# Moving the retention key projection behind product y in the third mixer problem of a two-layer encoder trunk

## The chip, the cores and the metric

The kernel runs on one core of one Trainium2 chip. The metric is the device time of one execution in microseconds (us), the median over several runs. Each run also has a profiled sibling, an execution recorded by the hardware profiler, from which every row below is taken. The engines are PE (matrix products; PEld is its weight load), DVE, ACT, POOL and SP, which issues most of the DMAs.

## What is computed

A trunk of two layers works on `x` of 512 positions by 1024 channels, in float32. Each layer is a token mixer and a gated feed-forward network, each followed by a layer norm. The mixer multiplies `x` by one wide matrix `w_in` and uses its columns for three branches:

```
h = x @ w_in[l]
rq, rk, rv, rg, cq, ck, cv, dq, dk, dv, gates = split(h)
o_a = silu(rg) * rmsnorm(retention(rotary(rq), rotary(rk), rv))   # 4 heads, keys of 128, values of 256
o_b = chunk_attention(cq, ck, cv)                                 # 8 heads of 64
o_c = diff_attention(rotary(dq), rotary(dk), dv)                  # 4 heads
merged = sum(sigmoid(gate_i) * (o_i @ w_branch_i));  x = layer_norm(a*x + merged @ w_out)
```

The change concerns the stretch in which `rk` of heads 2 and 3 and `rv`, `rg` of heads 2 and 3 are projected while the retention of heads 0 and 1 is finished.

## The kernel before, in words

Each float32 operand is carried as two float32r parts, a high part (a cast) and a low part (the rest), and each product is three matmuls (`mm3`, lines 121 to 124): high by high, high by low, low by high. A weight block of 128x2048 is loaded into a staging tile `st`, cast by ACT into `wh` (line 259 for whole blocks, 154 for blocks split in two halves), and subtracted by DVE into `wl` (lines 260 and 155).

Three pairs of wide projections of the mixer are **problems** called `w`, `p` and `q` (line 1114): `w` makes the values of branches b and c, `p` makes `rv` and `rg` of heads 0 and 1, and `q`, the last one, those of heads 2 and 3. Each problem is done with seven block products in place of eight (class `Close`, line 219, and `u_two`, line 733). The products are `m1`, `y`, `v`, `m2`, `x`, `g` and `h`. Some accumulate onto another's PSUM banks: `v` onto `y`'s, and `x` and then `g` onto `m1`'s. Before that happens ACT copies the bank out (`copy`, line 747; line 750 in the profile, `tc<-pf`). Each product has two halves, j=0 and j=1, each in one PSUM bank and each of 12 matmuls.

The operand names in the profile tell the products apart: `s12` is read by `y` and `x`, `s43` by `v` and `g`, `xT` in a `pf` product by `m1`, `m2` and `h`. `pt<-xT` is a plain projection such as the key block `rk` (`u_rqk`, line 681: 24 matmuls for each of two heads, then the rotation of lines 378 to 387 and a split).

The weight blocks of a problem are sums of quarters of the matrix. Block `a` (used by `y`) and block `c` (used by `g`) are put together by an accumulating DMA well ahead. `v` loads a quarter `d`, makes its block from it, and then adds `a` to it on DVE (line 233); `x` uses the sum. `m2` loads `e` and adds `d` to it (line 239); `h` uses that.

The mixer's work is a hand-written list of **items** (lines 1115 to 1131). An item is a weight block with the code that uses it, and up to two groups of small jobs, the first run after j=0 and the second after j=1 (`between`, line 549). The jobs here are one head's share of the retention: `s_dh` loads a decay table, `s_r1` makes scores (`psr`), `s_r2` multiplies them by the values (`pro`, 30 matmuls into two banks) and scales the result (DVE lines 833 and 840, with a power on POOL in between), and `s_r3` transposes that (`prt`, two banks) and splits it into `oa` (ACT line 108, DVE line 114).

Four pools set who has to wait for whom: `st` has 4 tiles, `wh` and `wl` have 3 each, there are 8 PSUM banks, and 61 general tiles (`NSTAGE`, `AHEAD`, line 66, `NSLOT`). `run_items` (line 555) fetches the block of item i+2 when item i begins, so that a cast waits for the block of item i-1 to be read to its end.

The program is not run in the order of this text: a scheduler at build time writes one fixed order for each engine, in which the order of the text is a priority and free tiles count. On the chip each engine then goes through its own fixed order. The rows of the prediction show places in which that order differs from the list.

Of the kernel before, what the change touches and what calls it, by code (L numbers as in the profile page):

```python
# [35 lines left out]
RQ, RK, RV, RG, CQ, CK, CV, DQ, DK, DV, GATE = (  # L36
    0, 512, 1024, 2048, 3072, 3584, 4096, 4608, 5120, 5632, 6144)
# [19 lines left out]
def trunk(ctx, tc, x_in, xT_in, w_in, ret_norm_g, da_norm_g, lq1, lk1, lq2, lk2, w_a, w_b, w_c, b_merge, w_out,  # L57
# [19 lines left out]
    def g(dt=F32, name="g"):  # L77
        return gp.tile([P, 512], dt, tag="g", name=name)
# [4 lines left out]
    def bank(name="ps"):  # L83
        return psp.tile([P, 512], F32, tag="ps", name=name)
# [15 lines left out]
    def triangle(name):  # L100

        return [Pair(name), Pair(name), HalfPair(name)]
# [13 lines left out]
    def split(pr, src, cols=slice(None), scale=None):  # L116

        part_hi(pr.hi[:, cols], src, scale)
        part_lo(pr.lo[:, cols], src, pr.hi[:, cols], scale)
# [226 lines left out]
    def proj_T(act, wt, c0, nk=KT, ps=None, half=None):  # L346

        ps = bank("pt") if ps is None else ps
        sl = slice(0, S) if half is None else slice(256 * half, 256 * half + 256)
        for k in range(nk):  # L350
            a = act[k]
            mm3(ps[:, sl], wt.hi[:, k, c0:c0 + P], wt.lo[:, k, c0:c0 + P], a.hi[:, sl], a.lo[:, sl],
                k == 0, k == nk - 1)
        return ps
# [194 lines left out]
    def between():  # L549

        if pending:
            for fn in pending.pop(0):
                fn()
# [54 lines left out]
    def layer(l):  # L608
# [4 lines left out]
        def wcols(c, n):  # L613
            return W[:, c:c + n]

        v = {}
# [51 lines left out]
        rq, rk, rv, rgt = {}, {}, {}, {}  # L668
# [7 lines left out]
        def rqk_done(dst, h, ps):  # L676
            r = rotary(ps, tabs["cr"], tabs["sr"], 64)
            dst[h] = Pair("rqk")
            split(dst[h], r)

        def u_rqk(dst, base, hp):
            def fn(wt):
                for j in range(2):
                    rqk_done(dst, 2 * hp + j, proj_T(xT, wt, P * j))
                    between()
            return [([wcols(base + 256 * hp, 256)], KT)], fn
# [99 lines left out]
        def s_dh(h):  # L786
            def fn():
                dhs[h] = g(name="dh")
                nc.sync.dma_start(dhs[h], decay[h])
            return fn  # L790

        def s_r1(h):
            def fn():
                dh = dhs.pop(h)
                rp[h] = triangle("rp")
                q, k = rq.pop(h), rk.pop(h)
                for b in range(3):
                    tmp = g(name="rtmp")
                    for mt in range(NT):
                        if PACK[mt][0] != b:  # L800
                            continue
                        o, w = PACK[mt][1], S - P * mt
                        ps = bank("psr")
                        msl = slice(P * mt, P * mt + P)
                        mm3(ps[:, :w], k.hi[:, msl], k.lo[:, msl], q.hi[:, P * mt:], q.lo[:, P * mt:], True, True)
                        nc.vector.tensor_mul(tmp[:, o:o + w], ps[:, :w], dh[:, :w])
                    w = PACKW[b]
                    split(rp[h][b], tmp[:, :w], cols=slice(0, w))
            return fn

        def s_r2(h):
            def fn():
                pT = rp.pop(h)
                hp, hc = h // 2, slice(256 * (h % 2), 256 * (h % 2) + 256)
                ss = small.tile([P, NT], F32, tag="ss", name="ss")
                banks = []
                for t2 in range(2):
                    ps = bank("pro")
                    banks.append(ps)
                    for j in range(2):  # L820
                        nt = 2 * t2 + j
                        for mt in range(nt + 1):
                            b, o = PACK[mt]
                            o += P * (nt - mt)
                            vp = rv[hp, mt]
                            mm3(ps[:, 256 * j:256 * j + 256], pT[b].hi[:, o:o + P], pT[b].lo[:, o:o + P],
                                vp.hi[:, hc], vp.lo[:, hc], mt == 0, mt == nt)
                    jk = g(name="junk")
                    for j in range(2):
                        nc.scalar.activation(jk[:, 256 * j:256 * j + 256], ps[:, 256 * j:256 * j + 256], AF.Square,  # L830
                                             accum_out=ss[:, 2 * t2 + j:2 * t2 + j + 1])
                rs = small.tile([P, NT], F32, tag="rsr", name="rsr")
                nc.vector.tensor_scalar(ss, ss, 4.0 / RET_DV, 4.0 * LN_EPS, op0=ALU.mult, op1=ALU.add)
                nc.gpsimd.tensor_tensor(rs, ss, mhalf, op=ALU.pow)
                os_ = []
                for t2 in range(2):
                    o = g(name="ro")
                    for j in range(2):
                        sl = slice(256 * j, 256 * j + 256)
                        nc.vector.scalar_tensor_tensor(o[:, sl], banks[t2][:, sl], rs[:, 2 * t2 + j:2 * t2 + j + 1],  # L840
                                                       rgt[hp, 2 * t2 + j][:, hc], op0=ALU.mult,
                                                       op1=ALU.mult)
                    os_.append(o)
                rps[h] = os_
            return fn

        def s_r3(h):
            def fn():
                os_ = rps.pop(h)
                for d in range(2):  # L850
                    ps = bank("prt")
                    for nt in range(NT):
                        nc.tensor.transpose(ps[:, P * nt:P * nt + P],
                                            os_[nt // 2][:, 256 * (nt % 2) + P * d:256 * (nt % 2) + P * d + P], ident)
                    oa[2 * h + d] = Pair("oa")
                    split(oa[2 * h + d], ps, scale=v["rg"][:, d:d + 1])
            return fn
# [30 lines left out]
        def u_cqk(p):  # L888
            def fn(wt):
                cqk[p] = QK()  # L890
                cqk[p].set_q(proj_T(xT, wt, 0), -CA_DH ** -0.5)
                between()
                cqk[p].set_k(proj_T(xT, wt, P))
            return [([wcols(CQ + P * p, P), wcols(CK + P * p, P)], KT)], fn
# [219 lines left out]
        w, p, q = u_two(Close(W, 0, 4, (CV, DV)), xq, v_away(cv, 64), v_away(dv, 128)), u_rvg(0), u_rvg(1)  # L1114
        for (specs, fn), *groups in [
            (u_first(),), (u_gate(0, 1), [s_q(0)], [s_q(1), w["a"]]), (w["m1"], [], [s_q(2)]), (u_gate(0, 2), [s_q(3), w["c"]]),
            (w["y"],), (w["v"],), (w["m2"], [lam]), (w["x"], [p["a"]]), (u_gate(0, 3),), (w["g"],), (w["h"], [p["c"]]),
            (p["m1"], [s_dh(0)]), (p["y"], [], [s_r1(0)]), (p["v"], [s_dh(1)]), (p["m2"], [], [s_r1(1)]),
            (p["x"], [q["a"]]), (u_rqk(rq, RQ, 1),), (p["g"], [q["c"]]), (p["h"],),
            (q["m1"], [], [s_r2(0)]), (u_rqk(rk, RK, 1), [s_r2(1)], [s_r3(0)]), (q["y"], [], [s_r3(1)]),  # L1120
            (q["v"], [s_dh(2)]), (q["m2"], [], [s_r1(2)]), (q["x"], [s_dh(3)]), (u_cqk(0), [], [s_r1(3)]), (q["g"],), (q["h"],),
            (u_gate(2, 0), [s_r2(2)], [s_r2(3), s_r3(2)]), (u_cqk(1), [s_r3(3)] + c(0)[0], c(0)[1]),
            (u_branch(0, 0), c(1)[0] + [v_back(cv)], c(1)[1]), (u_branch(0, 1), *c(2)), (u_cqk(2), *c(3)),
            (u_branch(0, 2), *c(4)), (u_cqk(3), *c(5)), (u_branch(0, 3), *c(6)), (u_gate(2, 1), *c(7)),
            (u_dqk(0), *c(8)), (u_gate(1, 0), [v_back(dv)], [s_c3(7)] + d(0)[1]), (u_branch(1, 0), *d(1)), (u_dqk(1),),
            (u_gate(1, 1), *d(2)), (u_branch(1, 1), *d(3)), (u_dqk(2),),
            (u_gate(1, 2), *d(4)), (u_branch(1, 2), *d(5)), (u_dqk(3),),
            (u_gate(1, 3), *d(6)), (u_branch(1, 3), *d(7)), (u_gate(2, 2), [s_d4(2)], [s_d2(3)]),
            (u_gate(2, 3), [s_d3(3)], [s_d4(3)]),
            (u_branch(2, 0),), (u_branch(2, 1),), (u_branch(2, 2),), (u_branch(2, 3),),  # L1130
        ]:
            item(specs, fn, *groups)
# [235 lines left out]
        p, q, o, w = u_fin(0), u_fin(1), fout_items(0), fout_items(1)  # L1368
# [73 lines left out]
```

## Time and profile before

| what | value |
|---|---|
| median of 3 runs | 1901.01 us (1900.52 to 1903.43) |
| profiled execution, its own time | 1905.45 us |
| span of its instructions | 1903.7 us |
| mean granted TensorE clock | 0.997 |
| DVE busy | 1290.6 us (68%) |
| ACT busy | 931.2 us (49%) |
| POOL busy | 114.0 us (6%) |

The profiled execution's own time is the one that its rows add up to; it is 4.44 us above the median of the three runs. A busy PE means that a matmul is in flight: neighbouring matmuls overlap, so the start of the next one tells more than the duration of one. In the rows of the timeline the columns are start, duration, engine, line, operation, output<-inputs, shape and count, and in brackets the idle time before it and what ended it. In the rows of stretches, the columns are the stretch, its length, the busy time of each engine with its count of instructions, the granted clock of PE and the DMA share.

### The profile page before, as it was taken

Reading aid. Unit: us, or ns where it says so; the run is one execution under the profiler, and the core shown is the slowest. Engines: PE = TensorE matmul, PEld = TensorE weight load, DVE = VectorE, ACT = ScalarE, POOL = GpSimd, SP = SyncE. Lnnn points to the kernel's source line nnn. Section 1 sums busy time; section 2 is a strip of 40 time slices with the busy share of each in tenths; the row PEclk is TensorE's granted clock in tenths of the full one; section 3 lists DMA queues with packets and bytes.
Section 4 is the critical chain, followed back from the end, with each engine's and each line's share of the span. In section 5 each row is a group of like instructions: output and inputs, shape, how many; then the busy total and the mean of one; then the engine's idle time right before and its main releaser. Section 6 shows DMA issues by size and latency. Waiting matters only on the chain. (4 is left out here: it accounts for less than half of the span.)

```text
span 1903.7 us, 24003 instructions
## 1 busy us (share of the span) xinstructions
PE 1886.1 (99%) x9170; PEld 1588.1 (83%) x9170; DVE 1290.6 (68%) x2047; ACT 931.2 (49%) x1547; POOL 114.0 (6%) x141
## 2 busy tenths in 40 slices
PE   9999999999999999999999999999999999999998
PEld 7888788888888888888898887888888888888886
DVE  6776766667766855775677767566776668467756
ACT  5545555567634444443355545545765344344430
POOL 2000000000000010000010000000000000000000
PEclk9999999999999999999999999999999999999999
DMA  9595344332155577766375844533322546876561
GB/s 282 151 285 150 119 141 128 111 119 81 56 173 160 154 172 179 202 155 155 111 201 171 273 111 122 171 108 109 122 67 77 189 121 165 189 181 185 144 154 44
DMA packets 239346, 285.09 MB, mean 150 GB/s; under 512 B 8580, under 2 KB 147936, under 8 KB 239232
## 3 DMA queue, kind: packets, MB, share of 16 engines
q1 hardware_dynamic: 215232, 237.01, 38.4%
q0 software_dynamic: 24000, 46.56, 14.5%
q8 instruction: 72, 1.18, 0.3%
q14 instruction: 42, 0.34, 0.1%
HBM read 260.42 MB, written 23.12 MB: 149 GB/s over the span
## 5 line engine op out<-in xcount | busy, mean ns | idle before, releaser
L122 PE MATMUL pt<-xTh,wh 128*128 128x512 f32 (+1 forms) x1328 | 498.3, 376 | 0.9 <-ACT wh L154 0.8
L124 PE MATMUL pt<-xTh,wl 128*128 128x512 f32 (+1 forms) x1328 | 494.4, 373 | 0.0
L123 PE MATMUL pt<-xTl,wh 128*128 128x512 f32 (+1 forms) x1328 | 494.3, 372 | 0.0
L155 DVE TENSOR_TENSOR wl<-st,wh 128x1024 fp32r<-128x1024 f32 (+1 forms) x236 | 257.2, 1113 | 102.0 <-ACT wh L154 87.4
L154 ACT CAST wh<-st 128x1024 fp32r<-128x1024 f32 (+1 forms) x236 | 220.2, 961 | 210.8 <-PE pt L123 84.4
L260 DVE TENSOR_TENSOR wl<-st,wh 128x2048 fp32r<-128x2048 f32 x98 | 224.6, 2292 | 122.1 <-ACT wh L259 121.1
L124 PEld LDWEIGHTS pt<-xTh,wl 128*128 128x128 f32 x1328 | 250.6, 189 | 43.9
L122 PEld LDWEIGHTS pt<-xTh,wh 128*128 128x128 f32 x1328 | 250.5, 189 | 43.3 <-ACT wh L154 1.5
L123 PEld LDWEIGHTS pt<-xTl,wh 128*128 128x128 f32 x1328 | 251.1, 189 | 41.8
L259 ACT CAST wh<-st 128x2048 fp32r<-128x2048 f32 x98 | 187.3, 1912 | 173.8 <-PE pt L123 73.9
L122 PE MATMUL pf<-wh,xTh 128*128 128x512 f32 x240 | 94.0, 392 | 0.4 <-ACT rph L106 0.4
L123 PE MATMUL pf<-wl,xTh 128*128 128x512 f32 x240 | 93.9, 391 | 0.0
L124 PE MATMUL pf<-wh,xTl 128*128 128x512 f32 x240 | 93.5, 390 | 0.0
L123 PE MATMUL pf<-wl,s12h 128*128 128x512 f32 x192 | 75.9, 395 | 3.2 <-DVE wl L260 3.2
L122 PE MATMUL pf<-wh,s12h 128*128 128x512 f32 x192 | 75.6, 395 | 2.2 <-ACT wh L259 2.2
L122 PE MATMUL pf<-wh,s43h 128*128 128x512 f32 x192 | 75.8, 395 | 0.0
L124 PE MATMUL pf<-wh,s12l 128*128 128x512 f32 x192 | 75.3, 393 | 0.0
L123 PE MATMUL pf<-wl,s43h 128*128 128x512 f32 x192 | 75.3, 392 | 0.0
L124 PE MATMUL pf<-wh,s43l 128*128 128x512 f32 x192 | 75.1, 391 | 0.0
L383 ACT COPY sw<-pt 32x512 f32<-32x512 f32 (+1 forms) x96 | 55.6, 579 | 33.0 <-PE pt L124 31.8
L1199 DVE TENSOR_TENSOR fth<-fth,pt 128x512 f32<-128x512 f32 x28 | 19.2, 687 | 68.7 <-PE pt L124 68.4
L750 ACT COPY tc<-pf 128x512 f32<-128x512 f32 x60 | 34.1, 586 | 54.2 <-PE pf L124 53.0
(341 smaller groups left out, 3494.4 us busy)
## 6 DMA issues: line engine op xcount, KB each, us to landing
st<-in_w_in SPq DMA_DIRECT2D x60, 1024.0 KB, 5.2
st<-in_w_ffn_in SPq DMA_DIRECT2D x56, 512.0 KB, 5.6
st<-in_w_ffn_out SPq DMA_DIRECT2D x20, 1024.0 KB, 5.1
st<-in_w_in SPq DMA_DIRECT2D x32, 512.0 KB, 5.1
st<-in_w_ffn_in SPq DMA_DIRECT2D x16, 1024.0 KB, 5.8
st<-in_w_ffn_in POOLq DMA_DIRECT2D x16, 1024.0 KB, 9.4
st<-in_w_ffn_out POOLq DMA_DIRECT2D x16, 1024.0 KB, 8.6
st<-in_w_in POOLq DMA_DIRECT2D x12, 1024.0 KB, 11.1
```

Source lines behind the costliest of these rows:

```text
L122: nc.tensor.matmul(ps, lh, rh, start=start, stop=False, skip_group_check=onto)
L123: nc.tensor.matmul(ps, lh, rl, start=False, stop=False, skip_group_check=onto)
L124: nc.tensor.matmul(ps, ll, rh, start=False, stop=stop, skip_group_check=onto)
L154: return [nc.scalar.copy(self.hi[:, a:b], self.st[:, a:b]), nc.vector.tensor_sub(self.lo[:, a:b], self.st[:, a:b], f(self.hi[:, a:b]))]
L155: nc.vector.tensor_sub(self.lo[:, a:b], self.st[:, a:b], f(self.hi[:, a:b]))]
L259: nc.scalar.copy(self.hi, st)
L260: nc.vector.tensor_sub(self.lo, st, f(self.hi))
L383: nc.scalar.copy(sw[half * b:half * b + half], ps[half * o:half * o + half])
L750: nc.scalar.copy(t[to, j], ps)
L1199: nc.vector.tensor_mul(t, t, pu)
```

## The change

In problem `q` the key block `u_rqk(rk, RK, 1)` stood between `m1` and `y`; it now stands between `y` and `v`. The jobs keep their order and move along by one item: `s_r2(1)` goes from the key block to `y`, after its first half; `s_r3(0)` stays on the key block, after its second half; and `s_r3(1)` goes from `y` to `v`, after its second half. The list is used by both layers, so this happens twice. No instruction's shape or operand changes.

```diff
             (p["x"], [q["a"]]), (u_rqk(rq, RQ, 1),), (p["g"], [q["c"]]), (p["h"],),
-            (q["m1"], [], [s_r2(0)]), (u_rqk(rk, RK, 1), [s_r2(1)], [s_r3(0)]), (q["y"], [], [s_r3(1)]),
-            (q["v"], [s_dh(2)]), (q["m2"], [], [s_r1(2)]), (q["x"], [s_dh(3)]), (u_cqk(0), [], [s_r1(3)]), (q["g"],), (q["h"],),
+            (q["m1"], [], [s_r2(0)]), (q["y"], [s_r2(1)]), (u_rqk(rk, RK, 1), [], [s_r3(0)]),
+            (q["v"], [s_dh(2)], [s_r3(1)]), (q["m2"], [], [s_r1(2)]), (q["x"], [s_dh(3)]), (u_cqk(0), [], [s_r1(3)]), (q["g"],), (q["h"],),
```

## The prediction made before the run

> **What bounds the kernel now.** I read the page first, for the bound.
>
> ```profile
> span 1903.7 us, 24003 instructions
> PE 1886.1 (99%) x9170; PEld 1588.1 (83%) x9170; DVE 1290.6 (68%) x2047; ACT 931.2 (49%) x1547; POOL 114.0 (6%) x141
> ```
>
> PE is the bound from end to end. The change adds and removes no matmul, so it can only change the time in which PE stands still or runs at a lower clock. The second view was the list of PE's waits, which is short.
>
> ```profile
> PE pf L123 <- DVE wl L260: 3.2, 2, 1.6
> PE pf L122 <- ACT wh L259: 2.2, 2, 1.1
> ```
>
> The two longest come twice each, so once in each layer. The third view, PE's timeline, says where in the first layer:
>
> ```profile
> 189.27 1.03 PE L853 MATMUL prt<-ident,ro 128*128 128x128 f32 x8
> 190.06 0.48 PE L122 MATMUL pf<-wh,s12h 128*128 128x512 f32 x1
> ...
> 195.60 1.03 PE L853 MATMUL prt<-ident,ro 128*128 128x128 f32 x8
> 197.75 0.73 PE L122 MATMUL pf<-wh,s12h 128*128 128x512 f32 x2 [1.11 <-ACT wh L259]
> 200.08 0.50 PE L123 MATMUL pf<-wl,s12h 128*128 128x512 f32 x1 [1.59 <-DVE wl L260]
> ...
> 201.81 0.39 PE L122 MATMUL pf<-wh,xTh 128*128 128x512 f32 x1
> ...
> 202.26 0.39 PE L122 MATMUL pf<-wh,s43h 128*128 128x512 f32 x1
> ```
>
> `y` runs from 190.06 to 195.60, s_r3(1) transposes follow, and then `v` (`s43`) is due by the list. It starts at 202.26. In between stand 9 matmuls of `x` and 2 of `m2`, both listed after `v`, and they wait for the block of `x`. So the question is why `v` was not put there. ACT's and DVE's timelines answer it:
>
> ```profile
> 189.24 1.91 ACT L259 CAST wh<-st 128x2048 fp32r<-128x2048 f32 x1 [3.38 <-PE pt L123]
> 191.17 1.18 ACT L383 COPY sw<-pt 64x512 f32<-64x512 f32 x2
> 195.80 1.90 ACT L259 CAST wh<-st 128x2048 fp32r<-128x2048 f32 x1 [3.46 <-PE pf L124]
> 197.61 0.61 ACT L106 CAST rqkh<-rot 128x512 fp32r<-128x512 f32 x1
> 198.13 1.26 ACT L108 ACTIVATE oah<-prt,colv 128x512 fp32r<-128x512 f32 x2
> 199.28 1.07 ACT L750 COPY tc<-pf 128x512 f32<-128x512 f32 x2
> ```
>
> ```profile
> 179.15 1.66 DVE L840 SCALAR_TENSOR_TENSOR ro<-pro,rsr,rg 128x256 f32<-128x256 f32 x4 [1.17 <-POOL rsr L834]
> ...
> 191.18 2.29 DVE L260 TENSOR_TENSOR wl<-st,wh 128x2048 fp32r<-128x2048 f32 x1 [2.33 <-ACT wh L259]
> ...
> 196.79 0.69 DVE L387 TENSOR_TENSOR rot<-rot,sw 128x512 f32<-128x512 f32 x1
> 197.73 2.29 DVE L260 TENSOR_TENSOR wl<-st,wh 128x2048 fp32r<-128x2048 f32 x1 [0.26 <-ACT wh L259]
> ...
> 200.54 2.72 DVE L114 SCALAR_TENSOR_TENSOR oal<-prt,colv,oah 128x512 fp32r<-128x512 f32 x4
> ```
>
> `v` accumulates onto `y`'s banks, so it needs ACT's two copies of `y`, `tc<-pf`. They run from 199.28 to 200.35, although `y` was done at 195.60 and its first half about 2.7 us sooner. On ACT they stand behind the cast at 195.80, which had to wait 3.46 us for `y` to leave its weight tile, behind the key block's last rotation (rqkh, at 197.61) and behind two splits of the head before. The copies are late because the key block's tail and `y` fall on ACT together.
>
> **What the stall costs.** The view of stretches gives both layers, the second stall at 1140.14:
>
> ```profile
> 195.60:202.26 6.66, 3.95 (x21) 2.89 (x19) 6.40 (x7) 5.72 (x8) 0.00 (x0) 1.00 0.16 38
> 1140.14:1148.62 8.48, 5.77 (x20) 4.23 (x19) 7.41 (x8) 5.71 (x8) 0.00 (x0) 0.72 0.35 112
> 202.26:207.70 5.44, 5.44 (x26) 4.51 (x24) 1.00 (x2) 0.59 (x1) 0.00 (x0) 1.00 0.56 195
> 1148.62:1155.06 6.44, 6.44 (x25) 5.22 (x24) 0.00 (x0) 0.59 (x1) 0.00 (x0) 0.84 0.18 58
> ```
>
> The pace of a matmul is the 24 of `v` in 5.44 us, 0.227 us each; eight transposes take 0.79 (189.27 to 190.06). The first stretch holds 8 transposes and 11 matmuls, 0.79 + 2.50 = 3.29 us of work, in 6.66: 3.37 us lost. In the second layer it is 8.48 - 3.29 = 5.19, and the 24 matmuls behind it take 6.44 in place of 5.44: 6.19 lost, 2.82 more than in the first layer. Those 2.82 us are clock (0.72 and 0.84 granted, 1.00 in the first layer), lost after the same wait. Together **9.56 us**: 6.74 of stall, 2.82 of clock.
>
> **The change part by part, first layer.** Nothing is added or removed, so each part is a question of what is ready when. The starts before:
>
> ```profile
> 171.15 0.28 PE L122 MATMUL pro<-rvh,rph 128*128 128x256 f32 x1
> ...
> 174.74 0.40 PE L122 MATMUL pt<-xTh,wh 128*128 128x512 f32 x1
> ...
> 180.21 0.28 PE L122 MATMUL pro<-rvh,rph 128*128 128x256 f32 x1
> ...
> 183.80 0.40 PE L122 MATMUL pt<-xTh,wh 128*128 128x512 f32 x1
> ```
>
> s_r2 takes 3.59 us, a half of the key block 5.47, a half of a product 2.73. With the new order: y j=0 174.7 to 177.5, s_r2(1) to 181.1, y j=1 to 183.8, keys to 189.3 and 194.7, s_r3(0) to 195.5, `v` to 201.0, s_r3(1) to 201.8, then `m2`. Now the parts.
>
> *y, moved forward.* Its block (made from `a`, no load of its own) takes the key block's place in the ring, so its cast falls where the key's did.
>
> ```profile
> 160.41 2.00 ACT L154 CAST wh<-st 128x1024 fp32r<-128x1024 f32 x2 [2.55 <-PE pf L124]
> ...
> 171.34 1.91 ACT L259 CAST wh<-st 128x2048 fp32r<-128x2048 f32 x1 [1.88 <-PE pf L124]
> ```
>
> ```profile
> 169.01 2.29 DVE L260 TENSOR_TENSOR wl<-st,wh 128x2048 fp32r<-128x2048 f32 x1 [1.11 <-ACT wh L259]
> ```
>
> With a subtraction of 2.29 us `y`'s block is ready by about 165 for 174.7; cost nothing. The key block takes `y`'s old place, whose subtraction is the one at 169.01, and is ready by about 171.3 for 183.8. `v`'s block is the cast at 171.34 in both orders, since both wait for `m1`. Without that cover, each would cost what it is late by; the smallest slack is about 10 us.
>
> *Loads on SP's queue.* The key block's staging tile comes free some 6 us later, and with it `e`'s load. It is needed for `m2`'s cast, now at 183.8 when `y` is done.
>
> ```profile
> 159.00 6.29 SPq L174 DMA_DIRECT2D st<-in_w_in  x2
> 177.97 22.45 SPq L150 DMA_DIRECT2D st<-in_w_in  x3
> ```
>
> ```profile
> st<-in_w_in SPq DMA_DIRECT2D x60, 1024.0 KB, 5.2
> ```
>
> `d` is the first of the pair at 159.00, `e` the second, at about 165; moved to 171.3 and with the page's 5.2 us to land, it is there at 176.5, 7 us early. The load at 177.97 waits for the add of `a`, which does not move. s_dh(2) stays on `v`; its table is for s_r1(2), a product and a half later. No DMA is passed.
>
> *s_r2(1), 2.7 us sooner on PE.* It needs two more banks: `m1` 2, first head 2, `y` 1, and these 2 make 7 of 8; y j=1 makes 8. The key's first half at 183.8 then needs the first head's banks, free when line 840 ends: 179.15 + 1.66 = 180.8. Slack 3.0 us; cost nothing.
>
> *The copies of y.* Ready from 177.5 and 183.8, when ACT has little to do, for `v` at 195.5: the stall goes, **3.37 us a layer**. Problem `p` shows the order in which it works, its `y` followed by 12 score matmuls and then `v`:
>
> ```profile
> 121.19 0.59 ACT L750 COPY tc<-pf 128x512 f32<-128x512 f32 x1 [0.26 <-PE pf L124]
> 123.91 0.59 ACT L750 COPY tc<-pf 128x512 f32<-128x512 f32 x1 [2.13 <-PE pf L124]
> ```
>
> ```profile
> 123.71 0.39 PE L122 MATMUL psr<-rqkh 128*128 128x512 f32 x1
> ...
> 125.61 0.39 PE L122 MATMUL pf<-wh,s43h 128*128 128x512 f32 x1
> ```
>
> Each copy follows its half at once and `v` waits for nothing, with 1.9 us between; the key block gives 11.
>
> *What is late next.* `m2` at 201.8 needs a bank, and `m1`, `v`, s_r3(0) and s_r3(1) hold all eight. One comes free when the first `oa` is split. The key block ends at 194.7; behind it the cast for `x` (1.90, to 196.6), its subtraction (2.29, to 198.9), three steps of the rotation at 0.69 (to 201.0), rqkh 0.61, oah 0.63 and oal 0.68 (to 202.9): 1.1 us late. With the rotation ahead of the subtraction, it begins after the two copies sw (1.18, to 197.8) and the same steps end at 201.8, in time. The trace does not show which; I take 0.6 a layer. It is bounded below by nothing, for a later wait can't speed PE up.
>
> Sum against the profiled execution: 1905.45 - 9.56 + 1.2 = 1897.1 us. The median of the timed runs is 4.44 below that execution, and these runs spread over 2.91 us, about one clock stretch of 2.82, so I don't know how many the median holds. I take the stall in full and half of one stretch: 1901.01 - 6.74 + 1.2 - 1.41 = 1894.06, **1894.0**.
>
> [...]
>
> **The rivals.**
> *No clock in the timed runs, or two stretches.* For it: only one of two equal stalls shows one. The stall with what is left of it is 6.74 - 1.2 = 5.54. Times 1901.01 - 5.54 = 1895.5, or less two times 2.82, 1889.8. These lie within the forecast.
>
> *The wait moves to m2.* The list is only a priority: before, `x` was put ahead of `v`. If the cast of the next item, `u_cqk(0)`, which waits for `v`'s end at 201.0, is put on ACT ahead of the splits as the cast at 195.80 was, then oah starts at 203.0 (two halves, 2.00), and with 0.63 and 0.68 the bank comes at 204.3, 2.5 us late a layer. Against it: the splits are ready at 195.5 and the copies of `v` free banks as well. Also here belongs that the emitted order keeps `v` late, so that the change does nothing. Time 1901.01 - 6.74 + 5.0 = 1899.3.
>
> *Slower: the key block waits for banks.* Place: the key's first half at 183.8. If DVE's line 840 of the first head is put behind the subtraction for `m2`, whose cast now waits for `y` at 183.8, its banks come at 183.8 + 1.9 + 2.3 + 1.7 = 189.7: 5.9 us a layer, 11.8 for 6.74 saved, 1906.1. It decides as soon as line 840 ends after 187.2 (3.4 us late). Against it: its inputs are ready near 179, and before it ran at 179.15.
>
> **How the numbers follow.** A measurement here tells about 0.2%, 3.8 us, from no change: faster is below 1897.2, slower above 1904.8. Forecast with its clock cases 0.66, all faster; the wait that moves 0.16, same; slower 0.18. The forecast alone spans 1889.8 to 1896.5 (two waits of 1.1 left, no clock: 1901.01 - 6.74 + 2.2). To leave out no more than 2 in 10, the range takes in the moved wait and the near part of the slower case: 1889.5 to 1903.5.
>
> **What would show it.** Right: `tc<-pf` of `y` well before `s43`; no `s12` ahead of it; PE's waits for `wh` and `wl` gone; granted clock 1.00 in both layers. Left over: a wait of about a microsecond of the first `m2` on `oal`. Wrong: a `pt` that waits for line 840, or `v` still behind `x`.

## The result and the profile after

| | before | after |
|---|---|---|
| median of 5 runs | 1903.43 us (1900.52 to 1905.14) | 1895.07 us (1894.74 to 1897.07) |
| ratio, 95% interval | | 0.9961 (0.9947 to 0.9976) |
| profiled execution, its own time | 1905.45 us | 1895.18 us |
| mean granted clock in it | 0.997 | 0.999 |

The changed kernel is faster, by 0.4%. By the ratio it saves 7.4 us (0.0039 x 1903.43), by its interval 4.6 to 10.1; the two medians alone differ by 8.4. The predicted saving was 7.0, from a base of 1901.01.

The head of the page after, with the same columns as before:

```profile
span 1893.4 us, 24003 instructions
PE 1880.3 (99%) x9170; PEld 1583.9 (84%) x9170; DVE 1291.3 (68%) x2047; ACT 932.4 (49%) x1547; POOL 114.1 (6%) x141
```

PE's three longest waits after (columns: total, times, longest), and the one row of before that is needed beside them:

```profile
PE warm L579 <- POOL ident masks.py:199: 1.5, 1, 1.5
PE pt L122 <- ACT wh L154: 1.0, 1, 1.0
PE pf L122 <- ACT rph L106: 0.8, 2, 0.4
```

```profile
PE pf L122 <- ACT rph L106: 0.4, 2, 0.2
```

The waits for `wl` (3.2 us) and `wh` (2.2 us) are gone. The two longest that are left come once, at the start of the program. The wait for `rph` (the high part of the scores), at the first matmul of `h`, was 0.2 us a layer and is 0.4.

PE's timeline after, in the first layer. Compare it with the order of before:

```profile
182.07 0.39 PE L122 MATMUL pt<-xTh,wh 128*128 128x512 f32 x1
...
192.95 1.03 PE L853 MATMUL prt<-ident,ro 128*128 128x128 f32 x8
193.74 0.48 PE L122 MATMUL pf<-wh,s43h 128*128 128x512 f32 x1
...
199.29 1.03 PE L853 MATMUL prt<-ident,ro 128*128 128x128 f32 x8
200.08 0.48 PE L122 MATMUL pf<-wh,s12h 128*128 128x512 f32 x1
...
202.75 0.47 PE L122 MATMUL pf<-wh,xTh 128*128 128x512 f32 x1
203.05 0.39 PE L123 MATMUL pf<-wl,xTh 128*128 128x512 f32 x1
```

The key block (`pt`) now begins at 182.07. `v` (`s43`) follows the transposes of s_r3(0) at once and no `s12` stands ahead of it. Ten matmuls of `x` (`s12`, 200.08 on) now fill the time between s_r3(1) and `m2` (202.75).

ACT's timeline after shows why `v` can start:

```profile
175.98 0.59 ACT L750 COPY tc<-pf 128x512 f32<-128x512 f32 x1 [1.94 <-PE pf L124]
...
182.27 0.59 ACT L750 COPY tc<-pf 128x512 f32<-128x512 f32 x1 [1.91 <-PE pf L124]
...
199.11 0.62 ACT L106 CAST rqkh<-rot 128x512 fp32r<-128x512 f32 x1 [3.08 <-DVE rot L387]
199.63 1.05 ACT L154 CAST wh<-st 128x1024 fp32r<-128x1024 f32 x1
200.58 0.69 ACT L108 ACTIVATE oah<-prt,colv 128x512 fp32r<-128x512 f32 x1
...
202.68 1.07 ACT L750 COPY tc<-pf 128x512 f32<-128x512 f32 x2
```

The second copy of `y` ends at 182.86, eleven microseconds ahead of `v`. The rows from 199.63 are what then stands before `m2`: one half of the cast of `cqk(0)`, the first block of chunk attention, did go ahead of the splits of `oa`, as a rival had it. The last row is the two copies of `v`. They too are late: `v`'s first half was done by about 196.6, ACT stood idle for 3.08 us up to 199.11, and the copies still came behind rqkh and two splits of `oa`.

DVE's timeline after has the row on which the banks of the key block depend:

```profile
177.39 1.66 DVE L840 SCALAR_TENSOR_TENSOR ro<-pro,rsr,rg 128x256 f32<-128x256 f32 x4 [1.17 <-POOL rsr L834]
```

Line 840 of the first head ends at 179.05, 3.0 us before the key block begins.

The stretch from the start of s_r2(0) to the first scores of s_r1(2), in both layers; first after, then before:

```profile
169.39:208.31 38.92, 38.77 (x208) 33.17 (x206) 26.65 (x31) 19.92 (x37) 2.06 (x2) 1.00 0.37 113
1110.87:1149.79 38.92, 38.77 (x207) 33.17 (x206) 26.65 (x31) 19.92 (x37) 2.05 (x2) 1.00 0.38 113
```

```profile
171.15:212.69 41.54, 38.83 (x207) 33.02 (x206) 25.77 (x31) 19.30 (x37) 2.06 (x2) 1.00 0.19 57
1115.68:1160.05 44.37, 41.66 (x206) 35.08 (x205) 25.78 (x31) 19.29 (x37) 2.05 (x2) 0.92 0.18 54
```

After, the stretch takes 38.92 us in both layers at a clock of 1.00, and holds one matmul of `x` more (ten ahead of `m2` in place of nine, 0.23 us). The first layer gained 41.54 - 38.92 + 0.23 = **2.85 us**, which is stall alone. The second gained 44.37 - 38.92 + 0.23 = **5.68 us**, which is the same 2.85 and 2.83 of clock. The longer wait of `h` takes back 0.2 a layer.

That is 8.1 of the 10.3 us between the two spans. Most of the rest isn't the change's. At the start of the program, which the change does not touch, the two executions differ; first before, then after:

```profile
4.70:12.00 7.30, 6.38 (x19) 4.35 (x18) 5.27 (x8) 4.47 (x8) 3.28 (x7) 1.00 1.02 312
```

```profile
4.70:12.00 7.30, 6.11 (x26) 4.34 (x25) 4.81 (x8) 4.33 (x7) 3.27 (x7) 1.00 1.02 314
```

In the same 7.30 us PE did 26 matmuls in place of 19, seven more, some 1.6 us at 0.227 each. About 0.6 us is left unassigned.

### The profile page after: what moved, and what is told of

Same layout as the page of the kernel before. It is cut to its first block, busy times and chain, and to the rows that moved or that the text cites. A ratio compares the mean times of both kernels' runs of the same rounds, so it can differ in the third digit from the quotient of the medians.

```text
span 1893.4 us, 24003 instructions
## 1 busy us (share of the span) xinstructions
PE 1880.3 (99%) x9170; PEld 1583.9 (84%) x9170; DVE 1291.3 (68%) x2047; ACT 932.4 (49%) x1547; POOL 114.1 (6%) x141
```

## The experiments

What was open. That the late copies of `y` held up `v` is one claim; why they were late is another. **The prediction's theory**: the key block's tail (its rotation, its last split) and `y` fall on ACT together, so ACT is busy when the copies are due, and distance between `y` and `v` cures it. **First rival**: the copies wait for a general tile. `tc` comes from the same pool as the tiles of the rotation and the split, and if tiles are handed out in the order of the text, the copies of `y` can't get theirs before the key block's last rotation and the splits of `oa` have theirs, however idle ACT is. **Second rival**: the moved jobs did it, not the moved block.

### jobs_alone: the last job moves, the key block stays

```diff
-(u_rqk(rk, RK, 1), [s_r2(1)], [s_r3(0)]), (q["y"], [], [s_r3(1)]),
-(q["v"], [s_dh(2)]),
+(u_rqk(rk, RK, 1), [s_r2(1)], [s_r3(0)]), (q["y"],),
+(q["v"], [s_dh(2)], [s_r3(1)]),
```

> The key block stays before y; only s_r3(1) leaves y for v. Queue theory (y's copies are late because the key block's tail and the cast for x stand ahead of them on ACT, and nothing lies between y and v): the copies still start near 199 and end near 200 in the first layer, PE still loses about 3.4 us a layer, time within 2 us of before. Tile theory (general tiles are handed out in the order of the text, so y's copies can't be placed before the key's rotated tile and the splits oa of s_r3(0)): the same. Rival, that it is the jobs and not the key block that count: the stall is gone, 5 to 9 us faster.

One run took 1904.0 us, beside 1904.53 for the kernel before (18 runs). PE's two long waits are those of before; the one for `rph` grew from 0.2 to 0.6 us at its longest:

```profile
PE pf L123 <- DVE wl L260: 3.2, 2, 1.6
PE pf L122 <- ACT wh L259: 2.2, 2, 1.1
```

Moving s_r3(1) does nothing by itself. The other moved job, s_r2(1), is left in place in the next kernel.

### key_alone: the key block moves, with its jobs

```diff
-(q["m1"], [], [s_r2(0)]), (u_rqk(rk, RK, 1), [s_r2(1)], [s_r3(0)]), (q["y"], [], [s_r3(1)]),
-(q["v"], [s_dh(2)]),
+(q["m1"], [], [s_r2(0)]), (q["y"],), (u_rqk(rk, RK, 1), [s_r2(1)], [s_r3(0)]),
+(q["v"], [s_dh(2)], [s_r3(1)]),
```

> The key block goes between y and v, s_r2(1) and s_r3(0) stay on it, so that y follows m1 and s_r2(0) with no job of its own. Queue theory and tile theory alike: as the changed kernel, the two waits of PE for wh and wl gone, 1894 to 1897 us. Rival, that the jobs count: the stall stays, 1900 to 1905.

1896.87 us, ratio 0.9965 (0.9952 to 0.9977). Both waits for the weight block of `x` are gone, and a small one came:

```profile
PE prt L853 <- DVE ro L840: 1.2, 2, 0.6
```

The moved block brings nearly all of the gain, so with jobs_alone the second rival falls. Left on the key block, s_r2(1) has only half a key block between itself and s_r3(0). Half of the first head's transposes then wait 0.6 us a layer for line 840 of the second head: they need a second bank, and by count that head holds it. So the job that the change moves to `y` is worth about that 1.2 us in the profile; the ratios of the two kernels, 0.9965 and 0.9961, don't tell them apart.

### own_tiles and slots59: the old order, with tiles of their own for the copies of y

The list is that of before. `y`'s two copies in problem `q` get a pool of two tiles; to keep the memory equal, the general pool has 59 tiles in place of 61 (the line that makes the new pool, `yp`, is left out of the diff). slots59 has only that second line and is the control.

```diff
-NSLOT = 61
+NSLOT = 59
...
-                    t[to, j] = g(name="t" + to)
+                    t[to, j] = yp.tile([P, 512], F32, tag="yc", name="tc22") if (hv.cols[0], to) == (RV + 512, "c22") else g(name="t" + to)
```

> The order of before; only the two copies of y in problem q take tiles of their own in place of general ones (59 general tiles are left for 61). Tile theory: the copies go ahead of the cast for x and of rqkh, done by about 196.5 in the first layer; v follows the transposes at once, the 3.4 us a layer are gone, and the time is 5 to 9 us below that of the kernel with 59 tiles alone. Queue theory: the key's tail and the casts are still on ACT at that time, the copies stay near 199, at most 1 us a layer is won.

> The order of before with 59 general tiles and nothing else, the control for the kernel with tiles of its own for y. Both theories: the stall stays, about 3.4 us a layer; time within 3 us of before.

own_tiles took 1898.16 us (1896.20 to 1898.30), ratio 0.9967 (0.9956 to 0.9977); slots59 took 1903.17 us (1902.62 to 1903.76), ratio 0.9995 (0.9986 to 1.0004). The tiles alone are worth 5.0 us, and no clock is in it: every timed run of both kernels has a granted clock of 0.998 or 0.999. ACT's timeline of own_tiles:

```profile
192.98 0.59 ACT L750 COPY tc<-pf 128x512 f32<-128x512 f32 x1 [0.73 <-PE pf L124]
195.71 0.59 ACT L750 COPY tc<-pf 128x512 f32<-128x512 f32 x1 [2.14 <-PE pf L124]
196.19 1.91 ACT L259 CAST wh<-st 128x2048 fp32r<-128x2048 f32 x1
198.00 0.62 ACT L106 CAST rqkh<-rot 128x512 fp32r<-128x512 f32 x1
```

and its PE:

```profile
195.51 1.03 PE L853 MATMUL prt<-ident,ro 128*128 128x128 f32 x8
196.30 0.48 PE L122 MATMUL pf<-wh,s43h 128*128 128x512 f32 x1
```

Key block, `y` and `v` stand as close as before, with the same cast and the same split on ACT, but each copy follows its half at once, now ahead of the cast and of rqkh, and `v` begins without a wait. ACT had idle time for the first of them all along: in the kernel before it stood idle for 3.46 us ahead of the cast at 195.80, and `y`'s first half was done about 2.7 us before its end. What the copies lacked was a tile.

The control keeps the stall in full:

```profile
PE pf L123 <- DVE wl L260: 3.2, 2, 1.6
PE pf L122 <- ACT wh L259: 2.3, 2, 1.2
...
PE pco L943 <- DVE cPl L112: 1.2, 2, 0.6
```

Two tiles fewer make the old waits hardly longer (they cost 0.6 us a layer elsewhere, at `pco` of the chunk attention, which own_tiles pays as well). So two tiles in the common pool don't matter and two kept for the copies do: what counts here is who gets a tile when one comes free. Whether many more common tiles would end the stall was not run.

### dve_copy: DVE copies y in place of ACT

```diff
-                    nc.scalar.copy(t[to, j], ps)
+                    (nc.vector.tensor_copy if (hv.cols[0], to) == (RV + 512, "c22") else nc.scalar.copy)(t[to, j], ps)
```

> The order of before; the two copies of y in problem q are done by DVE in place of ACT. Queue theory (what stands on ACT makes them late): freed of ACT's queue they run near 197.5 between DVE's steps of the rotation, v starts some 2 us sooner, 3 to 8 us faster. Tile theory (their tiles come after the key's rotated tile and two oa in the order of the text): on DVE too they stand behind rqkl and two oal, near 202, and PE loses as much as before or up to 2 us a layer more; time 1900 to 1908.

1903.76 us, ratio 0.9999 (0.9990 to 1.0008): no change. DVE's timeline:

```profile
194.82 0.69 DVE L387 TENSOR_TENSOR rot<-rot,sw 128x512 f32<-128x512 f32 x1
195.77 2.29 DVE L260 TENSOR_TENSOR wl<-st,wh 128x2048 fp32r<-128x2048 f32 x1 [0.26 <-ACT wh L259]
197.98 0.68 DVE L112 TENSOR_TENSOR rqkl<-rot,rqkh 128x512 fp32r<-128x512 f32 x1
198.58 1.40 DVE L114 SCALAR_TENSOR_TENSOR oal<-prt,colv,oah 128x512 fp32r<-128x512 f32 x2
199.90 1.28 DVE L750 COPY tc<-pf 128x512 f32<-128x512 f32 x2
```

On another engine the copies are just as late, and again behind the split of the key block and of `oa`. By itself this run is weak, because DVE is nearly full there (0.26 us idle in these rows). But the subtraction at 195.77 is for `x`, later in the list than `y`, and it went ahead of the copies although `y` was done at 193.64. Together with own_tiles, where ACT's work is the same and only the tiles differ, it speaks for the tiles and against ACT's queue.

### key_m1: the key block ahead of m1

`y` directly before `v`, with not even a job between, as in neither kernel, and the key block a product earlier.

```diff
-(q["m1"], [], [s_r2(0)]), (u_rqk(rk, RK, 1), [s_r2(1)], [s_r3(0)]), (q["y"], [], [s_r3(1)]),
-(q["v"], [s_dh(2)]),
+(u_rqk(rk, RK, 1), [], [s_r2(0)]), (q["m1"], [s_r2(1)], [s_r3(0)]), (q["y"],),
+(q["v"], [s_dh(2)], [s_r3(1)]),
```

> The key block goes ahead of m1: key, m1, y, v; s_r2(0) on the key block, s_r2(1) and s_r3(0) on m1, s_r3(1) on v. Nothing lies between y and v, and the key's tail is a product away from y. Queue theory in the form of the prediction (y and v must be kept apart): v still waits for the copy of y, 1 to 3 us lost a layer, x or m2 ahead of v again, time 1897 to 1902. Tile theory: nothing late stands before y's copies in the order of the text, they follow y's halves within a microsecond, PE loses under 0.7 us a layer, time 1894 to 1897.

1904.68 us, ratio 1.0008 (0.9999 to 1.0017). Both theories missed the time. PE's wait for the block of `x` shrank to 0.2 us a layer, but another came:

```profile
PE prt L853 <- DVE ro L840: 5.8, 2, 2.9
```

DVE's timeline shows it. The key block's rotation is late and cut in two, and the scaling of the first head stands behind it:

```profile
181.20 0.69 DVE L387 TENSOR_TENSOR rot<-rot,sw 128x512 f32<-128x512 f32 x1
...
189.39 1.66 DVE L840 SCALAR_TENSOR_TENSOR ro<-pro,rsr,rg 128x256 f32<-128x256 f32 x4 [1.17 <-POOL rsr L834]
```

Line 840 ends at 191.05 here, and 179.05 after the change. This is the mechanism of the prediction's slower rival, a late line 840, at another place and behind the rotation; here it costs 3 us a layer.

The copies of `y` missed the tile theory's expectation, that they follow `y`'s halves within a microsecond. ACT's timeline:

```profile
199.39 1.91 ACT L259 CAST wh<-st 128x2048 fp32r<-128x2048 f32 x1 [6.05 <-PE pf L124]
201.19 0.68 ACT L108 ACTIVATE oah<-prt,colv 128x512 fp32r<-128x512 f32 x1
201.78 1.07 ACT L750 COPY tc<-pf 128x512 f32<-128x512 f32 x2
```

`y`'s halves were done by about 196.5 and 199.2, and PE put half of `m2` and five matmuls of `x` ahead of `v`, as the queue theory expected of PE. But ACT stood idle for 6.05 us just before, so ACT's queue didn't hold the first copy. What stands ahead of the copies is a split of `oa` of s_r3(0), which in this text comes before `y` and was itself late. The expectation had overlooked that; a line for tiles in the order of the text fits these rows.

### cqk_between: another block between y and v

The old order, with the next plain projection between `y` and `v`; s_r1(3) goes to `g`.

```diff
-(q["y"], [], [s_r3(1)]),
+(q["y"], [], [s_r3(1)]), (u_cqk(0),),
...
-(q["x"], [s_dh(3)]), (u_cqk(0), [], [s_r1(3)]), (q["g"],),
+(q["x"], [s_dh(3)]), (q["g"], [], [s_r1(3)]),
```

> The key block stays before y, and another block, the first of chunk attention (48 matmuls, about 11 us), goes between y and v; s_r1(3) moves to g. y's copies stay behind the key's tail and the splits (near 199 to 200), but v is due only near 207. Queue theory and tile theory alike: no stall at v, 4 to 9 us faster. If what counts is that the key block is no longer ahead of y: the stall stays and the time is that of before.

1911.72 us, ratio 1.0045 (1.0029 to 1.0060). Both expectations missed it:

```profile
201.97 0.76 PE L122 MATMUL pt<-xTh,wh 128*128 128x512 f32 x1 [7.00 <-DVE oal L114]
202.53 0.63 PE L123 MATMUL pt<-xTl,wh 128*128 128x512 f32 x1
202.96 0.63 PE L124 MATMUL pt<-xTh,wl 128*128 128x512 f32 x1
```

There is no wait at `v` any more, but the block between needs a bank of its own, and by count `m1`, `y`, s_r3(0) and s_r3(1) hold 2 + 2 + 2 + 2, all eight. The first to come free is that of the first split `oa`, which on DVE stands behind the key block's tail and the sum for `m2`'s later block (line 239). PE waits for it 7.00 us in each layer. `v` needs no new bank, and the copies of `y` were done by 198.68 (197.61 + 1.07 on ACT), but PE's fixed order has nothing ahead of the block; in the kernel before, `x` filled part of the time. (Behind the wait the matmuls follow each other at 0.43 us, 202.53 to 202.96, in place of 0.227; the granted clock from 201.97 to 208.00 is 0.62.) So distance alone doesn't do it. What is put between must not itself wait for what the late tail holds, and the change meets that: its key block stands where the banks of the first head have been free for 3 us.

### r3_on_m2 and r3_and_r1: what is left over

The changed kernel, with s_r3(1) on `m2` in place of `v`, so that `m2` has its bank when it starts; the second kernel also has s_r1(3) half an item earlier, for the wait of `h`.

```diff
-(q["v"], [s_dh(2)], [s_r3(1)]), (q["m2"], [], [s_r1(2)]),
+(q["v"], [s_dh(2)]), (q["m2"], [s_r3(1)], [s_r1(2)]),
...
-(u_cqk(0), [], [s_r1(3)]),
+(u_cqk(0), [s_r1(3)]),
```

> The changed kernel with s_r3(1) moved on from v to m2, after its first half. What is left in the changed kernel is m2's wait for a bank that line 114 frees (0.15 us of waiting, 0.3 us of PE a layer) after ten matmuls of x were put ahead of m2. If the eight banks are the cause, two more are free here when m2 begins: no x ahead of m2, the wait gone, 0.6 us in all. If the bank is not the cause, m2 waits as before.

> As the kernel with s_r3(1) on m2, and s_r1(3) moved from behind the chunk-attention item to its middle, so that h no longer waits for the banks of the scores (0.4 us waited, 0.57 us of PE a layer in the changed kernel). Expected: that wait gone as well, about 1.7 us below the changed kernel in all, 1893 to 1894 us. Against it: s_r1(3) needs its decay table sooner, and its three splits fall beside the splits of q and k.

r3_on_m2 took 1894.15 us in one run; r3_and_r1 took 1896.74 us (1894.66 to 1897.34), ratio 0.9956 (0.9942 to 0.9969). In r3_on_m2 the wait of `h` is back at its old 0.2 us a layer, and `m2` follows `v` at once, with no `x` ahead of it:

```profile
198.78 0.39 PE L124 MATMUL pf<-wh,s43l 128*128 128x512 f32 x1
199.01 0.39 PE L122 MATMUL pf<-wh,xTh 128*128 128x512 f32 x1
```

So it was a bank that `m2` lacked in the changed kernel.

In r3_and_r1 the wait of `h` has given way to a longer one, which was not expected:

```profile
PE pf L122 <- DVE tc L765: 1.4, 2, 0.8
```

By its ratio r3_and_r1 isn't told apart from the changed kernel, and its expected 1893 to 1894 us was missed. The changed kernel and r3_on_m2 were then timed on one chip:

> The changed kernel once more, beside the two others of this call. Both theories: 1894.5 to 1897.5 us, PE's waits for wh and wl of block x gone, full clock in the third problem of both layers.

> The changed kernel with s_r3(1) on m2, now timed. Its one look showed no wait of m2 and a shorter one of h, so 0.6 to 1.0 us below the changed kernel; the intervals of the two will overlap.

The changed kernel took 1895.20 us (1894.16 to 1897.03), ratio 0.9956 (0.9944 to 0.9969), and r3_on_m2 1894.44 us (1893.46 to 1895.79), ratio 0.9951 (0.9939 to 0.9964). It is 0.8 us lower, about what the two waits are worth, but the intervals overlap: it isn't told apart from the changed kernel.

## Why the prediction was right, and where it was off

- **The stall** of `v` behind `x`: right: it was at `v`, it hung on the copies of `y`, and it is gone. Predicted 3.37 a layer less 0.6 left over, 2.77; measured 2.85 in the profile.
- **What is left at m2**: right in kind, and near in size. After, 202.75 - 200.08 = 2.67 us hold ten matmuls of `x`, 2.27 at 0.227, so 0.40 is lost there, and the first matmul of `m2` takes 0.08 more (202.75 to 203.05). That is about 0.5, as 3.37 - 2.85 says too, where 0.6 was taken as a middle between nothing and 1.1. The rival's mechanism, the cast of `cqk(0)` ahead of the splits, did happen; but only one half of it went ahead of the first split and the ten matmuls of `x` covered the rest. The prediction counted `x` as a loss of order when it stood ahead of `v`, and did not see that after the change the same matmuls cover the wait of `m2`.
- **The clock**: 2.83 us in the profiled execution against 2.82 predicted. Of the timed 7.4 us, the stall less `h`'s wait is 2 x 2.85 - 0.4 = 5.3, and 2.1 are left for clock and start-up; the prediction took 1.41. The 2.83 is no forecast that came true: it is the loss that the profile of before already showed, and what the run adds is that the profile after shows none. Half a stretch for the median was a guess, and that it came near is luck.
- **Bank slack of the key block** (3.0 us): right, 182.07 - 179.05 = 3.0. The slower rival did not come in this kernel, but key_m1 shows that it exists.
- **Blocks, loads, s_r2(1)** at nothing: right; no wait for any of them is in the list.
- **The wait of h for rph**, 0.2 a layer more: not foreseen.
- **The step that failed** is a reason, not a term of the sum: "The copies are late because the key block's tail and `y` fall on ACT together". The rows did show the copies behind the cast, rqkh and the splits; but the order of rows says only who came first, not why, and one of these rows had 3.46 us of idle ACT in it. own_tiles has the same tail on the same ACT and no stall, dve_copy has the copies off ACT and the full stall, slots59 has fewer tiles and the same stall. The copies stood in line for a general tile. That the line is the order of the text is argued, and not shown apart, from what comes ahead of the copies: rqkh or its low part and two splits of `oa` in before and in dve_copy, a split of `oa` in key_m1, and for the copies of `v` in the changed kernel rqkh and two splits again, the last two with 6.05 and 3.08 us of idle ACT. With this reason, the change works because `y` now asks for its tiles ahead of the key block, not because eleven microseconds lie between; and after the change it is `v` whose copies stand in that line. That the time came out right although the reason was wrong is luck in part: both reasons ask for the same move.

## What to carry to other kernels

When an operation is late on an engine that shows idle time before and after it, look for what it needs besides the engine: a tile from a pool that it shares with earlier code is such a need, and giving it two tiles of its own tests that with a few edited lines and here brought 5.0 us. Where something is put between a producer and its late consumer, first count the buffers that are held at that place, since a block that needed a ninth bank stood still for 7 us in each layer.

## What was not expected of the hardware

The same two waits (1.1 or 1.2 and 1.6 us with two matmuls between) went with a lowered clock in none, one or both layers: none in slots59, one in before (1.00 in the first layer, 0.72 in the second) and in jobs_alone (1.00 and 0.68), both in dve_copy. The two places in slots59, then in dve_copy:

```profile
194.50:201.50 7.00, 4.24 (x19) 3.04 (x18) 6.69 (x8) 5.36 (x8) 0.00 (x0) 1.00 0.27 85
1140.00:1147.00 7.00, 4.24 (x20) 3.03 (x19) 6.68 (x8) 5.28 (x8) 0.00 (x0) 1.00 0.27 90
```

```profile
194.40:204.00 9.60, 6.90 (x19) 4.96 (x18) 7.84 (x10) 4.18 (x6) 0.00 (x0) 0.65 0.42 137
1141.40:1150.40 9.00, 6.29 (x21) 4.56 (x20) 7.86 (x10) 4.20 (x6) 0.00 (x0) 0.81 0.44 146
```

Where it is lowered, matmuls follow each other at 0.43 us in place of 0.227 for about 6 us, and at the second place of dve_copy for about 3.4 (1146.17 to 1149.54). What decides in which layers this happens was not shown.

The start of the program, in the rows 4.70:12.00 of before and after, shows the same two paces. In before, matmuls follow each other at 0.43 us from 7.90 to 10.46 and at 0.227 from 10.79 on; in the changed kernel they do so at about 0.23 from 7.43 on. So 19 and 26 of them stand in the same first 7.30 us. The clock column read 1.00 in both of those rows, and for before also from 7.31 to 10.46, so at the start of this program the pace of the matmuls told more than the column.
